# Differential attention on one core: one rope and one split per head, the lambda factor on ScalarE, and the head norms' reciprocal roots seeded by Ln and Exp

## Chip, cores and metric

The kernel runs on one core of one Trainium2 chip. The metric is the device time of one execution in microseconds, lower is better. The kernel before was run three times: median 1824.09 us, between 1821.87 and 1824.63 us.

## The reference

One step of a diffusion backbone of two layers, over 128 context tokens and 512 latent tokens (640 in all) of width 1024, with 256 cached context positions. Layer 0 runs gated linear attention (GLA, 4 heads) beside latent attention (MLA, 4 heads); layer 1 runs differential attention (8 heads, two maps of 64 dimensions each); each is followed by a gated MLP with a width-3 convolution. What the change touches is this:

```python
def rmsnorm(x, g):
    y = xf * lax.rsqrt(jnp.mean(xf * xf, axis=-1, keepdims=True) + EPS)
    return y * g
def diff_attend(q, k, v, lam, scale):       # blocks of 128 queries
    s = jnp.einsum('bqhnd,bkhnd->bnhqk', qb, k) * scale
    p = jax.nn.softmax(s, axis=-1)
    a = p[:, 0] - lam * p[:, 1]
    return jnp.einsum('bhqk,bkhv->bqhv', a, v)
def diff_output(o, w_out, d_gain, lam_init):
    o = rmsnorm(o, d_gain) * (1.0 - lam_init)   # per head
    return o.reshape(b, t, MIX_ODD) @ w_out
# latent queries and keys pass axial_rope; context ones and cached ones don't
# GLA's output is normed per head in the same way: rmsnorm(o, gla_gain) * silu(gate)
```

## The kernel before, in words

**Number format.** Every float32 operand is kept as a high and a low part; `split` (ACT cast at L172, DVE subtraction at L173) makes them out of an SBUF tile, `evict_split` (ACT L177, DVE L178) out of a PSUM tile, `W` out of a weight that a DMA brought (`wraw`: ACT cast `whi` at L163, subtraction `wlo` at L165, on POOL in the attention of layer 1, on DVE elsewhere). A product is three matmuls (`three`). Weights stay still and tokens stream through, so one projection of a tile of 128 output features (`proj_half`, L211) takes 24 matmuls for one half of the tokens (two halves, 320 each).

**Order of work.** The program is emitted stage by stage: adaLN, input projection, GLA with MLA's first units between, MLA, output projection, MLP, then layer 1: norm (`nm_t`, `B`), the differential attention, its output projection (begun within the last head), MLP. Inside a stage a scheduler sorts each engine's instructions again, from its own estimate of when each is ready, so an edit of a few instructions moves others. Each engine runs its queue in order.

**The head norms.** `rms_stats` (L264 on) has per-head sums of squares in PSUM (PE `rb`, L261) with 64 tokens on the partitions and 8 or 10 columns. DVE makes `rv` (mean plus epsilon, L266), takes an integer guess at the reciprocal root (L267, L268) and refines it in three Newton rounds of three instructions (L270 to L272): 12 DVE instructions, each on the one before. `rms_bc` then spreads the result: DVE `rdg` (L278), PE `rbc` (L282). It runs 12 times: five times on GLA's output (64x8; three within GLA, two at MLA's start) and for seven of the eight differential heads (64x10).

**Queries and keys of layer 1.** `unit_qk(kind, h, c)` (L1060) projects queries or keys of head `h` for the token half `c`: PE `qko` (L211), ACT copy into `fq` or `fk` (L1076), then `rope` of the latent columns (DVE shuffle L478, DVE product with the sine L479, POOL product with the cosine L480, DVE sum L481), then `split` into `qd` or `kd` (L172, L173). The first half holds 192 latent columns, the second 320. For keys, the cached 256 columns (`in_dkc`) have a split of their own.

**A head's jobs.** Five jobs of 128 queries (four latent ones against 768 keys, one context job against 128), for each: scores of both maps (PE `sc`, L826), the minimum per map (DVE `mn`, L851), the exponential with its row sums (ACT `p`, L852), and one job later the reciprocal of the sums (DVE L862), `diff_maps` (L1097 to L1099: DVE multiplies the second map's factor by lambda; ACT scales map 0; DVE adds map 1 times its factor), the transposes (PE `ptp`, L869), their eviction `pt` (L177, L178) and the product with the values (PE `pv`, L883). `diff_after` (L1107 on) takes the result and norms the finished head. Projections of the next head, `unit_qk` and values `vo` (L1046), are dealt out between the jobs as filling.

Of the kernel before, what the change touches and what calls it, by code (L numbers as in the profile page):

```python
# [12 lines left out]
I32 = mybir.dt.int32  # L13
ACTF = mybir.ActivationFunctionType
ALU = mybir.AluOpType
# [6 lines left out]
CTX = 128  # L22
LAT = 512
TOK = CTX + LAT
CUT = 320
PAST = 256
ALLK = TOK + PAST
# [29 lines left out]
def build(tc, a):  # L57
    nc = tc.nc
    V, S, G, PE = nc.vector, nc.scalar, nc.gpsimd, nc.tensor

    def pool(name, bufs=1, **kw):
        es = ExitStack()
        return es.enter_context(tc.tile_pool(name=name, bufs=bufs, reuse_waits="tile", **kw)), es
# [38 lines left out]
    for n, sh in SMALL:  # L102
        w = math.prod(sh)
        v = small[:, off:off + w]
        off += w
        if len(sh) == 2:
            v = v.rearrange("p (a b) -> p a b", b=sh[1])
        elif len(sh) == 3:
            v = v.rearrange("p (a b c) -> p a b c", b=sh[1], c=sh[2])
# [7 lines left out]
    lm, dgn, epst, lnh = scal[:, 0:4], scal[:, 4:5], scal[:, 5:6], scal[:, 6:7]  # L117
# [19 lines left out]
    class Weights:  # L137
# [23 lines left out]
        def split(self, raw, shape, eng=None):  # L161
            hi = self.tile("hi", shape, FP32R)
            S.copy(out=hi, in_=raw)  # L163
            lo = self.tile("lo", shape, FP32R)
            (eng or self.eng).tensor_tensor(out=lo, in0=raw, in1=hi.bitcast(FP32), op=ALU.subtract)  # L165
            return hi, lo
# [8 lines left out]
    def evict_split(dst, ps_ap, scale=None):  # L175
        if scale is None:
            S.copy(out=dst[0], in_=ps_ap)  # L177
            return V.tensor_tensor(out=dst[1], in0=ps_ap, in1=dst[0].bitcast(FP32), op=ALU.subtract)  # L178
        S.mul(out=dst[0], in_=ps_ap, mul=scale)
        return V.scalar_tensor_tensor(out=dst[1], in0=ps_ap, scalar=scale, in1=dst[0].bitcast(FP32),  # L180
                                      op0=ALU.mult, op1=ALU.subtract)

    def three(x, y):
        return ((x[0], y[0]), (x[0], y[1]), (x[1], y[0]))
# [30 lines left out]
    mark = {}  # L215
# [32 lines left out]
    def rms_stats(tp, bank, srcs, denom):  # L248
        sizes = [s[0].shape[-1] // 64 for s in srcs]
        nb = sum(sizes)  # L250
        sums = bank[0:64, 0:2 * nb].rearrange("p (c t) -> p c t", t=2)
        b0 = 0
        for parts, n in zip(srcs, sizes):
            acc = tp.tile([128, CUT], FP32, tag="racc", name="racc")[:, 0:64 * n]
            S.activation(out=acc, in_=parts[0], func=ACTF.Square)
            for s in parts[1:]:
                sq = tp.tile([128, CUT], FP32, tag="rsq", name="rsq", bufs=2)[:, 0:64 * n]
                S.activation(out=sq, in_=s, func=ACTF.Square)
                mark["acc"] = V.tensor_tensor(out=acc, in0=acc, in1=sq, op=ALU.add)
            for c in range(n):  # L260
                PE.matmul(out=sums[:, b0 + c], lhsT=acc[:, c * 64:(c + 1) * 64], rhs=negs[:, 0:2], start=True, stop=True)  # L261
            b0 += n
        y = tp.tile([64, 20], FP32, tag="ry", name="ry")[:, 0:nb]
        v = tp.tile([64, 20], FP32, tag="rv", name="rv")[:, 0:nb]  # L264
        t = tp.tile([64, 20], FP32, tag="rt", name="rt")[:, 0:nb]
        V.tensor_scalar(out=v, in0=sums[:, :, 0], scalar1=-1.0 / denom, scalar2=EPS, op0=ALU.mult, op1=ALU.add)  # L266
        V.tensor_scalar(out=t.bitcast(I32), in0=v.bitcast(I32), scalar1=1, scalar2=None, op0=ALU.logical_shift_right)  # L267
        V.tensor_scalar(out=y.bitcast(I32), in0=t.bitcast(I32), scalar1=-1, scalar2=0x5F3759DF, op0=ALU.mult, op1=ALU.add)  # L268
        for _ in range(3):
            V.tensor_tensor(out=t, in0=y, in1=y, op=ALU.mult)  # L270
            V.scalar_tensor_tensor(out=t, in0=t, scalar=-0.5, in1=v, op0=ALU.mult, op1=ALU.mult)
            V.scalar_tensor_tensor(out=y, in0=t, scalar=1.5, in1=y, op0=ALU.add, op1=ALU.mult)  # L272
        return y

    def rms_bc(tp, bank, y, bufs=1, after=None, tag="rdg"):
# [199 lines left out]
    def rope(tp, z, t0=0):  # L475
        n, t1 = z.shape[0], t0 + z.shape[-1]
        sh = tp.tile([n, LAT], FP32, tag="rsh", name="rsh")[:, t0:t1]
        V.stream_shuffle(sh, z, SHUF)  # L478
        V.tensor_tensor(out=sh, in0=sh, in1=ropeS[0:n, t0:t1], op=ALU.mult)  # L479
        G.tensor_tensor(out=z, in0=z, in1=ropeC[0:n, t0:t1], op=ALU.mult)  # L480
        V.tensor_tensor(out=z, in0=z, in1=sh, op=ALU.add)  # L481
# [48 lines left out]
    for j, (src, gain) in enumerate(((cqr, sm["qn"]), (ckr, sm["kvn"]))):  # L530
        for h, (c0, c1) in enumerate(CH):
            bc = rms(scp, ps("p1", "rb"), [src[:, i, c0:c1] for i in range(2)], 256)
            for i in range(2):
                last = V.scalar_tensor_tensor(out=src[:, i, c0:c1], in0=src[:, i, c0:c1], scalar=gain[:, i:i + 1], in1=bc,
                                              op0=ALU.mult, op1=ALU.mult)
# [164 lines left out]
    def stats(c):  # L700
        RY[c] = rms_stats(scp, ps("m", "rb"), [[z] for z in OO[c]], 128.0)
# [16 lines left out]
    for i in range(2):  # L718
        V.tensor_tensor_reduce(out=ljk, in0=lamp[:, 2 * i], in1=lamp[:, 2 * i + 1], op0=ALU.mult, op1=ALU.add,
                               scale=1.0, scalar=0.0, accum_out=lm[:, i:i + 1])  # L720
# [310 lines left out]
    un, ues = pool("un", side="left")  # L1031
    dqt, dkt, dvt, doh = {}, {}, {}, {}

    def diff_units(p):
        us = {}
        wv = []

        def unit_v(t):
            if t == 0:
                wv.extend(W(a["wvo"][p, i], [128, 4, 256]) for i in range(2))  # L1040
            vt = dvt[p, t] = [vp.tile([128, 256], FP32R, tag=f"vd{i}", name=f"vd{i}", bufs=9) for i in range(2)]
            o_ = ps("p1", "vo")[:, 0:256]
            for k in range(KT):
                lh = [z[:, k, t * 128:(t + 1) * 128] for z in B]
                for n, (l_, r_) in enumerate(three(lh, wv[k // 4])):
                    PE.matmul(out=o_, lhsT=l_, rhs=r_[:, k % 4], start=k == 0 and n == 0, stop=k == KT - 1 and n == 2)  # L1046
            evict_split(vt, o_)
            if t == 0:
                vf = un.tile([128, 256], FP32, tag="vf", name="vf")
                V.tensor_copy(out=vf, in_=o_)  # L1050
                nc.gpsimd.dma_start(out=a["o_dv"][:, p * 256:(p + 1) * 256], in_=vf)

        def unit_c():
            vc = un.tile([128, 2, 256], FP32, tag="vc", name="vc")
            nc.gpsimd.dma_start(out=vc, in_=a["dvc"][:, :, p * 256:(p + 1) * 256])
            for t in range(2):
                vt = dvt[p, 5 + t] = [vp.tile([128, 256], FP32R, tag=f"vd{i}", name=f"vd{i}", bufs=9) for i in range(2)]
                split(vc[:, t], vt[0], vt[1])

        hold = {}  # L1060

        def unit_qk(kind, h, c):
            isq = kind == "q"
            n = TOK if isq else ALLK
            if c == 0:
                w = W(a["wqo" if isq else "wko"][h], [128, KT, 128])
                f = kp.tile([128, ALLK], FP32, tag="qkf", name="f" + kind, bufs=2)
                t = [kp.tile([128, n], FP32R, tag=f"{kind}d{i}", name=f"{kind}d{i}", bufs=2) for i in range(2)]
                (dqt if isq else dkt)[h] = t
                hold[kind, h] = (w, f, t)  # L1070
                if not isq:
                    nc.gpsimd.dma_start(out=f[:, TOK:ALLK], in_=a["dkc"][:, h])
            w, f, t = hold[kind, h]
            c0, c1 = CH[c]
            o_ = proj_half(ps("p1", "qko"), w, B, KT, c)
            S.mul(out=f[:, c0:c1], in_=o_, mul=-DIFF_SCALE if isq else 1.0)  # L1076
            if c == 0 and not isq:
                nc.gpsimd.dma_start(out=a["o_dk"][:, h], in_=f[:, 0:CTX])
                split(f[:, TOK:ALLK], t[0][:, TOK:ALLK], t[1][:, TOK:ALLK])
            r0 = max(c0, CTX)  # L1080
            rope(un, f[:, r0:c1], r0 - CTX)
            split(f[:, c0:c1], t[0][:, c0:c1], t[1][:, c0:c1])

        for t in range(5):
            us[f"v{t}"] = lambda t=t: unit_v(t)
        us["c"] = unit_c
        for j in range(2):
            for kind in "qk":
                for c in range(2):
                    us[f"{kind}{j}{'ab'[c]}"] = lambda kind=kind, j=j, c=c: unit_qk(kind, 2 * p + j, c)  # L1090
        return us
# [2 lines left out]
        return [three([z[m * 64:m * 64 + 64] for z in dqt[h]], [z[m * 64:m * 64 + 64] for z in dkt[h]]) for m in range(2)]  # L1094

    def diff_maps(p, li, nk):
        V.tensor_scalar(out=li[:, 1:2], in0=li[:, 1:2], scalar1=lm[:, 2:3], scalar2=None, op0=ALU.mult)  # L1097
        S.mul(out=p[:, 0, 0:nk], in_=p[:, 0, 0:nk], mul=li[:, 0:1])
        V.scalar_tensor_tensor(out=p[:, 0, 0:nk], in0=p[:, 1, 0:nk], scalar=li[:, 1:2], in1=p[:, 0, 0:nk],  # L1099
                               op0=ALU.mult, op1=ALU.add)  # L1100
        return p[:, 0]
# [253 lines left out]
```

## Time and profile before

| | |
|---|---|
| median of 3 runs | 1824.09 us (1821.87 to 1824.63) |
| the profiled execution | 1819.55 us |
| its span in the profile | 1817.8 us |
| instructions | 29362 |
| mean granted TensorE clock | 0.98 |
| busy: PE, DVE, ACT, POOL | 1744.3, 1272.0, 758.9, 294.7 us |

The profile is of one execution, 4.5 us under the median; what lies outside its span is 1.75 us. PE is TensorE's matmuls, PEld its weight loads, DVE VectorE, ACT ScalarE, POOL GpSimd. Stages on the profile's clock: GLA some 175 to 275 us, MLA to 385, output projection and MLP to 900, layer 1's norm to 950, differential attention 950 to 1300, the rest to the end. The granted clock is a mean over a stretch, 1.00 being 2.4 GHz; TensorE runs at 2.4 or at 1.2 GHz.

### The profile page before, as it was taken

Reading aid. Unit: us, or ns where it says so; the run is one execution under the profiler, and the core shown is the slowest. Engines: PE = TensorE matmul, PEld = TensorE weight load, DVE = VectorE, ACT = ScalarE, POOL = GpSimd, SP = SyncE. Lnnn points to the kernel's source line nnn. Section 1 sums busy time; section 2 is a strip of 40 time slices with the busy share of each in tenths; the row PEclk is TensorE's granted clock in tenths of the full one; section 3 lists DMA queues with packets and bytes.
Section 4 is the critical chain, followed back from the end, with each engine's and each line's share of the span. In section 5 each row is a group of like instructions: output and inputs, shape, how many; then the busy total and the mean of one; then the engine's idle time right before and its main releaser. Section 6 shows DMA issues by size and latency. Waiting matters only on the chain. (4 is left out here: it accounts for less than half of the span.)

```text
span 1817.8 us, 29362 instructions
## 1 busy us (share of the span) xinstructions
PE 1744.3 (96%) x11716; PEld 1634.6 (90%) x11716; DVE 1272.0 (70%) x2438; ACT 758.9 (42%) x1344; POOL 294.7 (16%) x246
## 2 busy tenths in 40 slices
PE   7999989999999999999999999999999999999996
PEld 1898776889999999999988989897989999999996
DVE  5964877778699999946588787876475554545556
ACT  6444434544532232323356665665373232322232
POOL 3201021000310100100133232321031010101004
PEclk9999999999999999999999989998999999999998
DMA  9650001044256555412231021111122222222121
GB/s 372 198 166 9 28 3 72 4 175 139 93 174 189 171 176 184 156 59 88 65 123 61 31 58 42 63 49 70 59 70 81 82 70 79 73 73 79 59 82 58
DMA packets 57336, 176.58 MB, mean 97 GB/s; under 512 B 6064, under 2 KB 11568, under 8 KB 56816
## 3 DMA queue, kind: packets, MB, share of 16 engines
q1 hardware_dynamic: 53408, 160.59, 27.4%
q0 software_dynamic: 3792, 14.13, 2.2%
q8 instruction: 92, 1.51, 0.3%
q14 instruction: 44, 0.36, 0.1%
HBM read 166.59 MB, written 7.77 MB: 96 GB/s over the span
## 5 line engine op out<-in xcount | busy, mean ns | idle before, releaser
L202 PE MATMUL up<-B,whi 128*128 128x320 f32 x2560 | 479.6, 309 | 0.0
L163 ACT CAST whi<-wraw 128x1024 fp32r<-128x1024 f32 (+2 forms) x208 | 208.3, 1002 | 506.7 <-PE up L202 231.3
L202 PEld LDWEIGHTS up<-B,whi 128*128 128x128 f32 x2560 | 401.6, 188 | 0.0
L165 DVE TENSOR_TENSOR wlo<-wraw,whi 128x1024 fp32r<-128x1024 f32 (+2 forms) x175 | 204.2, 1167 | 226.3 <-ACT whi L163 226.0
L202 PE MATMUL up<-B,wlo 128*128 128x320 f32 x1280 | 291.8, 309 | 0.0
L202 PE MATMUL po<-A,whi 128*128 128x320 f32 x1312 | 246.3, 310 | 0.7 <-DVE u L967 0.5
L202 PEld LDWEIGHTS up<-B,wlo 128*128 128x128 f32 x1280 | 213.8, 188 | 0.0
L363 DVE CUSTOM_DVE_ANT_0 junk<-araw,cbc 128x1024 bf16<-128x1024 f32 x160 | 203.5, 1272 | 12.2 <-DMA araw<-in_wada0b 9.4
L202 PEld LDWEIGHTS po<-A,whi 128*128 128x128 f32 x1312 | 205.7, 188 | 1.5 <-issue 0.7
L173 POOL TENSOR_TENSOR A<-u,A 128x640 fp32r<-128x640 f32 x44 | 76.1, 1730 | 758.2 <-ACT A L172 733.2
L202 PE MATMUL po<-A,wlo 128*128 128x320 f32 x656 | 149.8, 310 | 0.5 <-DVE wlo L165 0.5
L211 PE MATMUL qko<-B,whi 128*128 128x320 f32 x512 | 121.6, 322 | 2.4 <-ACT B L172 1.5
L340 PE MATMUL pot<-A,whi 128*128 128x320 f32 x512 | 113.9, 312 | 0.0
L202 PEld LDWEIGHTS po<-A,wlo 128*128 128x128 f32 x656 | 109.5, 188 | 0.8 <-DVE wlo L165 0.8
L165 POOL TENSOR_TENSOR wlo<-wraw,whi 128x1024 fp32r<-128x1024 f32 x33 | 79.1, 2400 | 146.9 <-ACT whi L163 146.5
L965 DVE SCALAR_TENSOR_TENSOR u<-up,small,u 128x127 f32<-128x127 f32 (+1 forms) x176 | 95.5, 543 | 10.4 <-ACT u L963 9.5
L967 DVE SCALAR_TENSOR_TENSOR u<-up,small,u 128x127 f32<-128x127 f32 (+1 forms) x176 | 96.3, 548 | 4.5
L852 ACT ACTIVATE p<-sc,mn 128x768 f32<-128x768 f32 (+1 forms) x100 | 79.2, 797 | 39.8 <-DVE mn L851 39.3
L211 PEld LDWEIGHTS qko<-B,whi 128*128 128x128 f32 x512 | 89.0, 196 | 5.2 <-ACT B L172 1.8
L851 DVE TENSOR_REDUCE mn<-sc 128x1 f32<-128x768 f32 (+1 forms) x100 | 79.3, 816 | 16.1 <-PE sc L826 15.3
L340 PEld LDWEIGHTS pot<-A,whi 128*128 128x128 f32 x512 | 85.7, 188 | 1.1 <-issue 0.4
L202 PE MATMUL pe<-B,whi 128*128 128x320 f32 x416 | 81.2, 317 | 4.3 <-DVE nm_t L306 3.6
(294 smaller groups left out, 3056.0 us busy)
## 6 DMA issues: line engine op xcount, KB each, us to landing
wraw<-in_wup SPq DMA_DIRECT2D x88, 512.0 KB, 3.6
araw<-in_wada SPq DMA_DIRECT2D x48, 512.0 KB, 3.4
wraw<-in_wdn SPq DMA_DIRECT2D x40, 512.0 KB, 3.6
araw<-in_wada0b SPq DMA_DIRECT2D x32, 512.0 KB, 4.3
wraw<-in_wie SPq DMA_DIRECT2D x13, 512.0 KB, 4.4
aw<-in_wada0a SPq DMA_DIRECT2D x8, 512.0 KB, 8.8
wraw<-in_wada0a SPq DMA_DIRECT2D x8, 512.0 KB, 8.0
wraw<-in_woe SPq DMA_DIRECT2D x8, 512.0 KB, 4.3
```

The lines of the kernel that those rows point to most:

```text
L163: S.copy(out=hi, in_=raw)
L165: (eng or self.eng).tensor_tensor(out=lo, in0=raw, in1=hi.bitcast(FP32), op=ALU.subtract)
L173: return (lo_eng or V).tensor_tensor(out=lo, in0=src, in1=hi.bitcast(FP32), op=ALU.subtract)
L202: PE.matmul(out=o, lhsT=w[wi][:, k], rhs=hl[ri][:, k, c0:c1], start=k == 0 and n == 0, stop=k == nk - 1 and n == 2)
L211: PE.matmul(out=o, lhsT=w[wi][:, k], rhs=hl[ri][:, k, c0:c1], start=k == 0 and n == 0, stop=k == nk - 1 and n == 2)
L340: PE.matmul(out=o, lhsT=ws[j + m][wi][:, k], rhs=hl[ri][:, k, c0:c1], start=k == 0 and n == 0, stop=k == nk - 1 and n == 2)
L363: V.tensor_tensor_reduce(out=junk, in0=raw, in1=self.cbc[:, j], op0=ALU.mult, op1=ALU.add, scale=1.0, scalar=0.0, accum_out=mods[l][:, t0 ...
L851: V.tensor_reduce(out=mn[:, m:m + 1], in_=ss[m][:, 0:nk], op=ALU.min, axis=AX.X)
L852: self.exp = S.activation(out=p[:, m, 0:nk], in_=ss[m][:, 0:nk], func=ACTF.Exp, scale=-1.0, bias=mn[:, m:m + 1], accum_out=li[:, m:m + 1])
L965: V.scalar_tensor_tensor(out=u[:, s0 + 1:s1], in0=r[:, s0:s1 - 1], scalar=cw[:, 0:1], in1=u[:, s0 + 1:s1], op0=ALU.mult, op1=ALU.add)
L967: last = V.scalar_tensor_tensor(out=u[:, s0:s1 - 1], in0=r[:, s0 + 1:s1], scalar=cw[:, 2:3], in1=u[:, s0:s1 - 1], op0=ALU.mult, op1=ALU.add)
```

## The change

Three edits. In `rms_stats` the two integer instructions and two of the three Newton rounds go; ACT computes the start as Ln and then Exp with a scale of -0.5, and one round stays. In `unit_qk` the rope and the split are issued once per head and kind, when both halves are there: the rope over 512 columns, the split over 640 for queries and over 896 for keys (the cached columns with them). In `diff_maps` the lambda factor is an ACT instruction instead of a DVE one.

```diff
@@ rms_stats
-        V.tensor_scalar(out=t.bitcast(I32), in0=v.bitcast(I32), scalar1=1, scalar2=None, op0=ALU.logical_shift_right)
-        V.tensor_scalar(out=y.bitcast(I32), in0=t.bitcast(I32), scalar1=-1, scalar2=0x5F3759DF, op0=ALU.mult, op1=ALU.add)
-        for _ in range(3):
-            V.tensor_tensor(out=t, in0=y, in1=y, op=ALU.mult)
-            V.scalar_tensor_tensor(out=t, in0=t, scalar=-0.5, in1=v, op0=ALU.mult, op1=ALU.mult)
-            V.scalar_tensor_tensor(out=y, in0=t, scalar=1.5, in1=y, op0=ALU.add, op1=ALU.mult)
+        with tc.issue_after(mark["tab"].ins):
+            S.activation(out=t, in_=v, func=ACTF.Ln)
+            S.activation(out=y, in_=t, func=ACTF.Exp, scale=-0.5)
+        V.tensor_tensor(out=t, in0=y, in1=y, op=ALU.mult)
+        V.scalar_tensor_tensor(out=t, in0=t, scalar=-0.5, in1=v, op0=ALU.mult, op1=ALU.mult)
+        V.scalar_tensor_tensor(out=y, in0=t, scalar=1.5, in1=y, op0=ALU.add, op1=ALU.mult)
@@ unit_qk
             if c == 0 and not isq:
                 nc.gpsimd.dma_start(out=a["o_dk"][:, h], in_=f[:, 0:CTX])
-                split(f[:, TOK:ALLK], t[0][:, TOK:ALLK], t[1][:, TOK:ALLK])
-            r0 = max(c0, CTX)
-            rope(un, f[:, r0:c1], r0 - CTX)
-            split(f[:, c0:c1], t[0][:, c0:c1], t[1][:, c0:c1])
+            if c == 1:
+                rope(un, f[:, CTX:TOK])
+                split(f[:, 0:n], t[0], t[1])
@@ diff_maps
-        V.tensor_scalar(out=li[:, 1:2], in0=li[:, 1:2], scalar1=lm[:, 2:3], scalar2=None, op0=ALU.mult)
+        S.mul(out=li[:, 1:2], in_=li[:, 1:2], mul=lm[:, 2:3])
```

`mark["tab"]` orders Ln and Exp behind the load of the activation table that both are in; the number of table loads is the same in both kernels. The changed file is one line shorter, so lines from L1083 on are one less there: the lambda factor is L1096, ACT's scaling of map 0 L1097, DVE's sum L1098. PE has the same matmuls in another order. Three places of its queue show it.

PE at MLA's start, where the last GLA chunk's norm is spread (`rbc`) among MLA's projections (`uq`, `uv`) and products with values (`pv`). Before:

```order
L883 MATMUL pv<-pt_2780,B_65 128x256
L883 MATMUL pv<-pt_2781,B_65 128x256
L883 MATMUL pv<-pt_2780,B_65 128x256 x2
L883 MATMUL pv<-pt_2781,B_65 128x256
L883 MATMUL pv<-pt_2780,B_65 128x256
L282 MATMUL rbc<-rdg,negs 128x256 x2
L795 MATMUL uv<-wv_2674,B_66 128x256
```

In the change:

```order
L282 MATMUL rbc<-rdg,negs 128x256
L211 MATMUL uq<-cqn_1570,whi 128x320
L211 MATMUL uq<-cqn_1571,whi 128x320
L211 MATMUL uq<-cqn_1570,wlo 128x320
...
L883 MATMUL pv<-pt_2751,B_65 128x256
L883 MATMUL pv<-pt_2750,B_65 128x256
L282 MATMUL rbc<-rdg,negs 128x256
L795 MATMUL uv<-wv_2644,B_66 128x256
```

The two `rbc` stood next to each other behind `pv`; now six `uq` and nine `pv` stand between them.

PE at the entry of the differential attention, where the first head's scores (`sc`; `kd` and `qd` with the two numbers are the high and low parts of its keys and queries) stand among the projections `qko` of the second head's keys. Before:

```order
L211 MATMUL qko<-B_65,wlo 128x320
L826 MATMUL sc<-kd_9143,qd_9233 128x512 x2
L211 MATMUL qko<-B_65,wlo 128x320
L826 MATMUL sc<-kd_9144,qd_9233 128x512 x2
L826 MATMUL sc<-kd_9143,qd_9234 128x512 x2
L826 MATMUL sc<-kd_9143,qd_9233 128x256 x2
L826 MATMUL sc<-kd_9144,qd_9233 128x256 x2
L826 MATMUL sc<-kd_9143,qd_9234 128x256 x2
L211 MATMUL qko<-B_65,whi 128x320
L211 MATMUL qko<-B_66,whi 128x320
```

In the change:

```order
L211 MATMUL qko<-B_65,whi 128x320
L211 MATMUL qko<-B_66,whi 128x320
L211 MATMUL qko<-B_65,wlo 128x320
L826 MATMUL sc<-kd_9113,qd_9194 128x512 x2
L826 MATMUL sc<-kd_9114,qd_9194 128x512 x2
L826 MATMUL sc<-kd_9113,qd_9195 128x512 x2
L826 MATMUL sc<-kd_9113,qd_9194 128x256 x2
L826 MATMUL sc<-kd_9114,qd_9194 128x256 x2
L826 MATMUL sc<-kd_9113,qd_9195 128x256 x2
L826 MATMUL sc<-kd_9113,qd_9194 128x512
L826 MATMUL sc<-kd_9114,qd_9194 128x512
```

Before, 22 of the 46 `qko` stood behind the first job's first scores, 21 of them between the first job and the second. Now all 46 stand ahead of the first score, and 30 `sc` (the first job's 12, the second's 12, half of the third's) follow one another.

PE at the end of a head (here the second; the fourth and sixth have the same), behind the context job's scores and the norm's `rbc`. Before:

```order
L282 MATMUL rbc<-rdg,negs 128x320 x2
L826 MATMUL sc<-kd_10378,qd_10600 128x512
L826 MATMUL sc<-kd_10379,qd_10600 128x512
L826 MATMUL sc<-kd_10378,qd_10601 128x512
L826 MATMUL sc<-kd_10378,qd_10600 128x256
L826 MATMUL sc<-kd_10379,qd_10600 128x256
L826 MATMUL sc<-kd_10378,qd_10601 128x256
L869 MATMUL ptp<-small,p 128x128 x3
```

In the change:

```order
L282 MATMUL rbc<-rdg,negs 128x320 x2
L869 MATMUL ptp<-small,p 128x128 x6
L883 MATMUL pv<-pt_10650,vd_10127 128x256
L211 MATMUL qko<-B_65,whi 128x320
L211 MATMUL qko<-B_66,whi 128x320
```

Where 12 `sc` of the next head's first job stood, there are now the transposes, a `pv` and 22 `qko`; the scores follow behind them.

## Rows read from the trace of the kernel before

**Rows 1.** The page: busy time by engine, and the chain that ended last by engine.
```profile
PE 1744.3 (96%) x11716; PEld 1634.6 (90%) x11716; DVE 1272.0 (70%) x2438; ACT 758.9 (42%) x1344; POOL 294.7 (16%) x246
PE 40%; DVE 4%; ACT 3%; issue 1%; DVEq 0%; ACTq 0%
```

**Rows 2.** Windows by stage. Columns: window, its length, busy time (instructions) of PE, PEld, DVE, ACT and POOL, granted clock, DMA share, GB/s.
```profile
175.00:275.00 100.00, 90.73 (x746) 72.74 (x745) 79.74 (x208) 41.83 (x99) 15.89 (x18) 1.00 0.06 19
900.00:950.00 50.00, 46.47 (x307) 44.14 (x306) 42.91 (x93) 29.73 (x67) 14.20 (x18) 0.97 0.30 105
950.00:975.00 25.00, 23.18 (x146) 21.20 (x145) 21.10 (x39) 15.90 (x31) 9.73 (x9) 0.86 0.16 52
975.00:1235.00 260.00, 252.90 (x1870) 231.88 (x1868) 205.77 (x475) 157.79 (x350) 78.39 (x64) 0.97 0.16 50
1235.00:1300.00 65.00, 59.17 (x355) 52.77 (x354) 35.36 (x79) 29.16 (x63) 5.27 (x9) 0.87 0.19 65
```

**Rows 3.** Short windows, same columns: one of GLA, and five of the differential attention (its entry, and places at the end of heads).
```profile
200.00:225.00 25.00, 22.86 (x189) 18.56 (x187) 22.53 (x59) 12.54 (x29) 0.00 (x0) 1.00 0.00 1
960.00:972.00 12.00, 10.18 (x58) 9.29 (x57) 10.30 (x19) 9.94 (x19) 4.18 (x3) 0.72 0.13 44
1052.00:1060.00 8.00, 6.00 (x48) 5.29 (x48) 7.07 (x12) 3.56 (x9) 4.25 (x4) 0.88 0.51 163
1064.00:1076.00 12.00, 11.48 (x55) 9.41 (x54) 9.50 (x22) 7.16 (x18) 3.52 (x2) 0.72 0.16 45
1138.00:1148.00 10.00, 7.99 (x60) 7.36 (x57) 9.31 (x22) 5.18 (x12) 3.69 (x4) 0.83 0.33 107
1220.00:1228.00 8.00, 7.08 (x54) 6.38 (x55) 6.95 (x19) 4.65 (x12) 2.96 (x2) 0.84 0.33 104
```

**Rows 4.** Timeline of DVE in GLA, a norm's Newton instructions among GLA's own. Columns here and in the other timelines: start in us, duration in us, engine, line, operation; in brackets the idle time before it and what ended it.
```profile
224.48 0.15 DVE L270 TENSOR_TENSOR rt<-ry 64x8 f32<-64x8 f32 x1
224.56 0.72 DVE L667 COPY_PREDICATED sT<-lmask,gp 128x512 f32<-128x512 uint32 x1
225.55 0.16 DVE L270 TENSOR_TENSOR rt<-ry 64x8 f32<-64x8 f32 x1
225.74 0.16 DVE L271 SCALAR_TENSOR_TENSOR rt<-rt,rv 64x8 f32<-64x8 f32 x1
```

**Rows 5.** Timelines of DVE and of PE at MLA's start, the last GLA chunk's norm.
```profile
296.75 0.16 DVE L266 TENSOR_SCALAR rv<-rb 64x8 f32<-64x8 f32 x1 [0.31 <-PE rb L261]
299.90 0.42 DVE L278 TENSOR_TENSOR rdg<-nid,ry 64x256 f32<-64x256 f32 x1
300.38 0.70 PE L282 MATMUL rbc<-rdg,negs 64*128 64x256 f32 x2 [0.73 <-DVE rdg L278]
301.97 0.69 PE L282 MATMUL rbc<-rdg,negs 64*128 64x256 f32 x2 [0.90 <-DVE rdg L278]
```

**Rows 6.** Timeline of the entry of the differential attention, the first two jobs of the first head and the wait ahead of the third.
```profile
954.38 0.50 PE L826 MATMUL sc<-kd,qd 64*128 64x512 f32 x2
956.91 1.81 DVE L851 TENSOR_REDUCE mn<-sc 128x1 f32<-128x768 f32 x2
957.89 0.90 ACT L852 ACTIVATE p<-sc,mn 128x768 f32<-128x768 f32 x1 [2.05 <-DVE mn L851]
959.43 1.90 PE L826 MATMUL sc<-kd,qd 64*128 64x512 f32 x12
963.15 3.31 PE L826 MATMUL sc<-kd,qd 64*128 64x512 f32 x12 [1.82 <-ACT p L852]
```

**Rows 7.** First PE's waits from 900 to 1310 us (line, what it waited for: us in total, times, longest), then rows of the timeline at ends of heads.
```profile
PE pv L883 <- DVE pt L178: 6.7, 5, 2.0
PE sc L826 <- ACT p L852: 4.3, 6, 1.8
985.77 1.30 PE L826 MATMUL sc<-kd,qd 64*128 64x512 f32 x6 [0.86 <-ACT p L852]
1053.02 3.48 DVE L1099 SCALAR_TENSOR_TENSOR p<-p,li 128x768 f32<-128x768 f32 x1 [0.93 <-ACT p L1098]
1053.32 2.36 POOL L165 TENSOR_TENSOR wlo<-wraw,whi 128x1024 fp32r<-128x1024 f32 x1
1067.41 1.51 PE L826 MATMUL sc<-kd,qd 64*128 64x512 f32 x6 [0.52 <-ACT p L852]
1152.85 1.31 PE L826 MATMUL sc<-kd,qd 64*128 64x512 f32 x6 [0.52 <-ACT p L852]
```

**Rows 8.** Groups of instructions by form from 944 to 1290 us. Columns: line, engine, operation, names, shapes, count; busy us, mean ns; idle us before them and what ended it.
```profile
L1097 DVE TENSOR_SCALAR li<-li,scal 128x1 f32<-128x1 f32 x40 | 8.4, 211 | 0.8
L1099 DVE SCALAR_TENSOR_TENSOR p<-p,li 128x768 f32<-128x768 f32 x32 | 42.4, 1326 | 14.3 <-ACT p L1098 14.1
L479 DVE TENSOR_TENSOR rsh<-rsh,ropeS 128x320 f32<-128x320 f32 x16 | 17.6, 1097 | 0.1
```

**Rows 9.** One line's instructions over the whole span, those whose size the change uses or comes near to. Columns: line, engine, operation, count; duration in ns (lowest, median, highest); first and last start in us; shapes.
```profile
L478 DVE STREAM_SHUFFLE rsh<-qrf x2: 724/734/743, 273.9 to 318.3; 128x512 f32<-128x512 f32 x2
L480 POOL TENSOR_TENSOR qrf<-qrf,ropeC x2: 1284/1289/1294, 274.7 to 319.1; 128x512 f32<-128x512 f32 x2
L173 DVE TENSOR_TENSOR krs<-kr,krs x1: 1093/1093/1093, 118.1 to 118.1; 128x896 fp32r<-128x896 f32 x1
L172 ACT CAST csr<-csil x1: 206/206/206, 6.7 to 6.7; 128x16 fp32r<-128x16 f32 x1
```

## The prediction, made before the changed kernel was run

> **What bounds the kernel now.** I read the page first: PE is busy 96% of the span, and the chain that ended last lies on PE far more than on any other engine [rows 1]. So an instruction taken from DVE or ACT is worth nothing by itself; it is worth what PE stands still for it. Next the windows by stage, for where PE does stand still [rows 2]. In GLA it is busy 90.7 us of 100, and DVE there 22.5 of 25 us in a typical stretch [rows 3]: DVE sets the pace. In the differential attention PE has 252.9 of 260 us, DVE 205.8: PE sets the pace, and DVE only at places. PE loses there in two ways: 7 us idle, and the granted clock, 0.97 of full speed on average and 0.86 and 0.87 at entry and end. A stretch's clock loss I take as (1 - granted clock) x length: at the lower of its two levels, 1.2 GHz, the engine needs twice as long. Last the waits of PE and the timelines at those places [rows 5 to 7], to see whose work ends them.
>
> **The change, part by part.** The sum is made against the profiled execution, 1819.55 us, and carried over to the median, 1824.09; the two are 4.5 us apart, so the difference counts, not the profile's own time.
>
> *Newton rounds in GLA.* Three norms lose 8 of 12 DVE instructions each. One standing alone behind another starts 0.19 us after it; one slipped behind a long instruction of another chain adds 0.08 (it starts at 224.48 and the next at 224.56) [rows 4]. With half of each kind that is 8 x 0.13 = 1.05 us, three times 3.1. DVE is the engine that sets the pace, so I count all of it: -3.1. The bounds are 0 (the chunk's chain runs over ACT's exponentials anyway) and 3 x 8 x 0.19 = -4.6. Ln and Exp stand on ACT behind exponentials that are due earlier and ahead of casts; ACT is busy 41.8 of 100 us [rows 2] and covers them; without that cover, two at the 0.206 us of a small cast [rows 9] would cost 0.4 a norm.
>
> *MLA's start.* The norm of the last chunk is a bare chain here: from `rv` at 296.75 to `rdg` at 299.90 it is 3.15 us, and PE waits 0.73 and 0.90 for the two `rdg` [rows 5]. Without 8 links of 0.19 and with two of 0.2 the chain is 1.1 us shorter or more, and the new order puts six `uq` and nine `pv` between the two spreads. Both waits go: -1.6. The bounds are 0, if something else is late at the same places, and -2.7, if the 1.1 us come on top. Layer 1's norm is not touched; its stage has 3.5 us of PE idle [rows 2], and its order shifts a little: 0, plus or minus 1.
>
> *Entry of the differential attention.* Now the first score starts at 954.38, the 21 projections behind the first job cover its minima and exponentials, the second job starts at 959.43 without a wait, and only the third waits, 1.82 us [rows 6]. In the new order all 46 projections come first and nothing stands between the jobs. The 22 that move forward take as long in front as behind, and cover the whole rope and the longer splits, so the first score starts near 957.5 and nothing is lost yet. Then the scores of a map need their PSUM tile back, which the job before frees by minimum and exponential. Ahead of the second job PE waits for a shuffle of the next head's rope (0.73) [rows 9], two minima (1.81 together) and an exponential (0.90) [rows 6], 3.5 in all, less 1.1 that lie beside the scores' own second half: 2.4. Ahead of the third, DVE also has the rest of that rope and the 896-column split of the keys (1.09), the sine product held up by POOL's cosine product of 1.29 [rows 9] as it is now with 320 columns, which take 1.10 [rows 8]: 3.2. A last wait makes 0.3. Together 5.9 instead of 1.8: **+4.1**. The bounds: 0, if the scheduler's order is right and the engines are ready; and three waits of the full 2.7 (two minima and one exponential) and the 0.73, 8.8 less 1.8: +7.0. Behind today's wait the clock falls: 0.72 over 12 us, 3.4 us lost [rows 3]. Two longer waits may bring it down twice; I take half of a second such loss, **+1.7**, between 0 and +3.4.
>
> *Ends of heads.* PE waits 0.86, 0.52 and 0.52 for the context job's exponential, as the next scores need its PSUM tile [rows 7]. In the new order transposes, a `pv` and projections stand there at the last two and something like it at the first: the waits are filled, -1.9. After the second of them the clock is at 0.72 for 12 us [rows 3]; if the wait is what lets it fall, that comes back too, **-3.4**; the bounds are 0 and -3.4. The other waits, 6.7 us for the eviction of the transposes [rows 7], I leave. The DVE sum at L1099 takes 3.48 us in front of that eviction instead of 1.33 on average [rows 7, 8], because POOL's `wlo` of 2.36 runs at the same time, and the change moves neither. The longer key split and the lambda instruction now stand in front, +0.2 each at three places: +0.6.
>
> *Lambda and the rest.* DVE loses 40 lambda instructions, 8.4 us [rows 8], seven norms' 8 links, and some work of the two-part ropes. All of that lies under PE's 252.9 of 260 us [rows 2] and I cost it at nothing. If PE's cover breaks at some job, the freed DVE time is a gain, not a loss; ACT's side is a rival below. The last head, where the clock is 0.87 [rows 2], has a new order too: 0, plus or minus 2.
>
> The sum: -3.1 - 1.6 + 4.1 + 1.7 - 1.9 - 3.4 + 0.6 = **-3.6 us**, 1820.5 as a median.
>
> **The lambda factor and a rule.** For a small ACT instruction this case has 0.206 us [rows 9], for the DVE one 0.211 [rows 8]: by the rows the move is even, and what counts is which queue it stands in. The Trainium skill, page "ScalarE: Activation LUTs", section "Rules for kernel authors", says of products: "Use VectorE, not ScalarE". The same page, section "What ACT_TABLE_LOAD costs", gives an ACTIVATE 186 ns and 93 ns more for each per-partition operand: an estimate of 0.28 us here, 40 x 0.28 = 11 us instead of the 8.2 of the last rival if all lay on the path. By that rule the edit should be undone; no row of this kernel shows the form itself.
>
> **Rivals.**
>
> *Larger gain.* The waits for the eviction go as well, since DVE has fewer instructions in its queue at the ends of heads, and with them the clock losses there: 8 x 0.12 + 10 x 0.17 + 8 x 0.16 = 4.0 us [rows 3]. Then -3.6 - 0.6 - 6.7 - 4.0 = -14.9: 1809.2. For it: DVE is busy 7.07 of 8 us and 9.31 of 10 there. Against: what delays the eviction is the one slow sum beside POOL, which stays.
>
> *It does nothing that counts.* The scheduler places the work so that what DVE gives back in GLA is waited for at ACT's exponentials, while entry and ends cancel as forecast: -3.6 + 3.1 = -0.5, 1823.6. For it: PE is at 96%, and each gain hangs on a place of 0.5 to 1 us.
>
> *Slower at the entry.* The one mechanism is the chain of three jobs of scores without filling. If every job waits the full chain, +7.0, and each wait is followed by a stretch at the lower clock, +3.4, and no gain comes at the ends (+0.6): -4.7 + 7.0 + 3.4 + 0.6 = +6.3, 1830.4. It decides once the waits at the entry pass about 6 us in all. For it: the order has nothing between the scores, and the clock now falls behind one wait of 1.8 us. Against: it is one place in the program, and later heads keep their filling.
>
> *Slower by ACT's queue.* The lambda factor stands between the second exponential and the scaling of map 0, for which the DVE sum already waits 14.1 us [rows 8]. If each of 40 goes straight into PE's time at 0.206 us, that is +8.2 on the forecast: +4.6, 1828.7. Against: PE has other work at most of these places.
>
> **How the numbers follow.** Forecast 0.50, larger gain 0.13, nothing 0.15, slower at the entry 0.17, slower by ACT 0.05. The forecast's own range is 1815 to 1825: the clock's 3.4 at the ends and the entry's 4.1 can each fail to come. The whole range, 1810 to 1831, takes in all but the far half of the larger gain and the upper half of the slower entry. A measurement of this kernel can tell about 0.2%, 3.6 us, from no change. The forecast lies on that edge: of its 0.50 I put 0.28 on faster and 0.22 on same; the larger gain adds 0.13 to faster; the third case gives 0.11 to same and 0.02 to each side; the slow ones 0.21 to slower and 0.01 to same. Faster 0.43, same 0.34, slower 0.23.
>
> **What would show it.** In the changed kernel's profile: GLA's stage about 3 us shorter with DVE still near 90%; no wait of `rbc` for `rdg` at MLA's start; the first score some 3 us later on the stage's own clock and two waits of `sc` for `p` between 2 and 3.5 us behind it; no such wait behind the context jobs of heads two and four; waits of `pv` for `pt` still near 2 us. The prediction is wrong in its mechanism if GLA keeps its length, if the entry has no wait longer than today's, or if the change of time lies in the stages in front of or behind 175 to 1300 us.

## The result: slower where the forecast had faster

The changed kernel takes 1831.90 us (median of 6 runs, 1829.26 to 1837.21); the kernel before, run again beside it, 1821.83 us (6 runs). The ratio is 1.0061, 95% interval 1.0041 to 1.0081: some 11 us slower where 3.6 us faster was forecast, and 0.9 us above the range. Its profiled execution took 1830.81 us, span 1829.0 us, mean granted clock 0.979 against 0.980.

The windows by stage of the changed kernel, with the columns of [rows 2]:

```profile
175.00:275.00 100.00, 93.28 (x755) 74.75 (x754) 75.92 (x183) 43.38 (x108) 14.97 (x19) 1.00 0.07 20
950.00:975.00 25.00, 20.56 (x106) 17.77 (x105) 17.07 (x24) 16.37 (x31) 7.82 (x6) 0.73 0.12 33
975.00:1235.00 260.00, 249.76 (x1828) 227.70 (x1826) 178.05 (x309) 159.29 (x363) 73.29 (x49) 0.97 0.16 50
1235.00:1300.00 65.00, 58.26 (x326) 50.20 (x325) 34.77 (x68) 31.82 (x77) 7.89 (x10) 0.83 0.14 49
```

DVE gave back 28 us in the long window, and PE did not get any: it is busy less, not more. In GLA it is busy 2.5 us more in the same 100 us, which is part of the gain ahead of layer 1.

Windows with fixed ends mix the stages once a kernel runs ahead or behind, so the stages are better measured from the first and the last instruction of a line. For the changed kernel (line, operation, count; ns lowest/median/highest; first and last start; shapes):

```profile
L826 PE MATMUL sc<-kd,qd x432: 269/383/792, 951.6 to 1271.3; 64*128 64x256 f32 x65, 64*128 64x512 f32 x63, 64*128 64x128 f32 x16
L950 PE MATMUL po<-A,whi x96: 303/309/555, 1245.7 to 1303.9; 128*128 128x320 f32 x96
L202 PE MATMUL up<-B,whi x2560: 309/309/309, 473.9 to 1783.7; 128*128 128x320 f32 x197
```

The same rows of before begin or end at 954.4, 1292.5 and 478.8 to 1772.5 us. GLA's first matmul starts at 183.6 us instead of 182.4. So from there to the first MLP matmul the change gains 6.1 us; from the first differential score to the last output projection it loses 14.2 (338.1 to 352.3), and 3.2 more, as the 22 projections moved ahead of that first score are no longer in it; the rest is even.

Within the differential stage I split the time in three, the same way for each trace: PE's waits (the brackets of its timeline), the clock's loss ((1 - granted clock) x length, in windows of 4 us), and what is left.

| profile | stage | waits | clock | left |
|---|---|---|---|---|
| before | 338.1 | 14.2 | 20.4 | 303.5 |
| the change | 352.3 | 21.2 | 25.6 | 305.5 (+3.2) |

So of 17.4 us there, 7.0 are waits, 5.2 clock, and 5.2 neither. The waits of PE from 900 to 1310 us, which answer to the first two of [rows 7]:

```profile
PE sc L826 <- ACT p L852: 5.8, 4, 2.6
PE ptp L869 <- DVE pt L178: 3.8, 8, 0.6
PE pv L883 <- ACT pt L177: 3.2, 4, 1.0
PE qko L211 <- DVE doh L1124: 2.1, 2, 1.2
PE po L950 <- ACT A L172: 2.0, 1, 2.0
PE pv L883 <- DVE pt L178: 1.7, 3, 0.6
```

The 6.7 us behind the slow DVE sum fell to 1.7, and new lines stand there: transposes wait for evictions, projections for the norm (`doh`), products with the values for ACT.

One name has to be set right before these places are read. What the section on the change calls the end of the second head (and of the fourth and sixth) is where the third, fifth and seventh head run their last jobs; the norm that PE spreads there (`rbc`) is that of the second, fourth and sixth head. Below, the place goes by the head whose jobs end there.

### The profile page after: what moved, and what is told of

It reads as the page before. It is cut to its first block, busy times and chain, and to the rows that moved or that the text cites. A ratio compares the mean times of both kernels' runs of the same rounds, so it can differ in the third digit from the quotient of the medians.

```text
span 1829.0 us, 29148 instructions
## 1 busy us (share of the span) xinstructions
PE 1752.2 (96%) x11716; PEld 1638.8 (90%) x11716; DVE 1241.8 (68%) x2214; ACT 768.7 (42%) x1384; POOL 288.1 (16%) x230
```

## Experiments

Each was timed in five rounds beside the kernel before; the difference is that of the medians. The change itself, counted the same way, stands at +10.1.

| run | edit against before | ratio (95%) | us |
|---|---|---|---|
| e1_ln | Ln and Exp only | 0.9949 (0.9931 to 0.9967) | -9.4 |
| e2_rope | merged rope and split only | 1.0122 (1.0100 to 1.0144) | +22.7 |
| e3_lam | lambda on ACT only | 1.0042 (1.0026 to 1.0059) | +8.2 |
| e4_lnlam | both ACT edits | 0.9963 (0.9946 to 0.9980) | -6.8 |
| e5_head0 | the change, first head in halves | 1.0070 (1.0046 to 1.0095) | +14.0 |
| e6_lnrope | the change, lambda on DVE | 1.0098 (1.0075 to 1.0121) | +19.3 |
| e7_pair_after | the change, scores in turns | 1.0100 (1.0076 to 1.0124) | +18.5 |
| e8_ln_pair | e1, scores in turns | 0.9976 (0.9962 to 0.9990) | -5.0 |
| e9_qonly | the change, only queries merged | 1.0094 (1.0077 to 1.0111) | +18.1 |
| e10_konly | the change, only keys merged | 0.9983 (0.9970 to 0.9997) | -3.1 |
| e11_ropelam | merged, and lambda on ACT | 1.0116 (1.0098 to 1.0133) | +22.4 |
| e12_ln_gla | Ln and Exp for GLA's norms only | 0.9961 (0.9947 to 0.9975) | -5.4 |
| e13_ln_fill | e1 with matmuls in three waits | 0.9914 (0.9897 to 0.9932) | -16.7 |
| e14_ln_nolam | e1 without lambda | 0.9945 (0.9925 to 0.9965) | -11.3 |
| e15_qfirst | the change, queries dealt out first | 1.0158 (1.0134 to 1.0182) | +28.2 |

### Which edit: e1 to e4

The edits are those of the diff, one or two at a time.

> The Ln and Exp seed alone, rope, split and lambda as before. Theory 1 (the merged rope and split make the loss, through a new order of PE's queue in the differential attention): only the gain in GLA and at MLA's start is left, about 6 us in the two traces, the differential stage keeps its 338 us from the first score to the last output projection; about 6 us faster than before. Theory 2 (ACT is late: the added ACT instructions delay the exponentials and the evictions at the ends of heads): the same 6 us gained, 4 or more of them lost at the ends of heads; within 2 us of before.

> One rope and one split per head alone, norms and lambda as before. Theory 1: the whole loss of the differential stage without the gain ahead of it, entry +6, ends of heads +5, scores of the two maps run apart +4: some 14 to 17 us slower than before, first wait of scores behind the first job near 2.6 us. Theory 2: the entry's 6 only, since ACT has no new instruction here: about 6 us slower, and no wait of products with the values for an ACT eviction.

> The lambda factor on ACT alone. Theory 1: no more than 2 us either way, the order of PE's scores hardly differs from before (14 jobs of 768 keys paired, as before). Theory 2: 40 instructions of some 0.2 us in ACT's queue, 4 to 8 us slower, waits of products with the values for ACT's eviction at the ends of heads.

> Both ACT edits, the rope and split in halves as before. Theory 1: about 6 us faster than before, as with Ln and Exp alone. Theory 2: the gain of 6 eaten by ACT's delays, within 3 us of before or slower.

The merge is the loss, +22.7 us, more than theory 1 had. Ln and Exp gain 9.4, more than the 6 ahead of the differential stage: that stage is 5.2 us shorter too (332.9 us). Of these 22.7 us, 19.0 lie in the differential stage (357.1 us): 5.6 more of waits and 13.7 more of clock loss. Theory 2 had the size of lambda, which costs 8.2 us by itself; the 2.6 beside Ln and Exp lie within the two intervals. In e3_lam, lambda's line on ACT (columns as above):

```profile
L1097 ACT ACTIVATE li<-li,scal x40: 282/296/321, 962.3 to 1270.2; 128x1 f32<-128x1 f32 x40
```

and who waited there for the scaling of map 0 behind it (us, times):

```profile
  DVE p L1099: 21.6, 26
```

One takes 0.296 us where I put the 0.206 of a small cast, and the sum waits 21.6 us instead of 14.1 [rows 8]. PE's waits in the stage hardly rise (14.2 to 14.7 us), and the waits for ACT's eviction that theory 2 expected are not among them; the clock loss rises (20.4 to 25.6).

### Where: e5 to e8

```diff
 e5: unit_qk of the change
+            if h == 0:          # cached split, rope and split by halves, as before
...
+            elif c == 1:
                 rope(un, f[:, CTX:TOK])
                 split(f[:, 0:n], t[0], t[1])
 e6: diff_maps of the change
-        S.mul(out=li[:, 1:2], in_=li[:, 1:2], mul=lm[:, 2:3])
+        V.tensor_scalar(out=li[:, 1:2], in0=li[:, 1:2], scalar1=lm[:, 2:3], scalar2=None, op0=ALU.mult)
 e7, e8: s_stage of the change and of e1
+            prev = None
             for grp in zip(*ops):
                 for f in grp:
-                    mark["att"] = f()
+                    with tc.issue_after(prev.ins) if prev and nm == 2 else ExitStack():
+                        prev = mark["att"] = f()
```

> The change, but the first head's queries and keys keep rope and split in halves, so that PE's queue at the entry is the one of before (22 of 46 projections behind the first job's first scores); the ends of heads stay as in the change. Theory 1 (the entry costs its waits, 2.6 us more, and a longer stretch at the low clock, 3.4 us more): about 6 us faster than the change, near 1826 us, no wait of scores longer than 2 us at the entry. Rival (the loss is at the ends of heads alone, and the clock falls there instead when it does not at the entry): within 2 us of the change.

> The change with the lambda factor on DVE as before. Alone the lambda edit cost some 8 us in time; theory 1: its 40 instructions of 0.29 us lie in front of the scaling of map 0 in every job here too, 6 us or more faster than the change, near 1826. Rival: at the ends of heads PE waits for ACT's eviction and the merged splits anyway, lambda is covered by these, within 2 us of the change.

> The change, with each differential job's scores held in the order map 0, map 1, map 0, ... by ordering edges alone, so that no other work stands between the maps and neighbours come from different maps. Theory 1 (a job whose maps run apart takes PE 2.5 us, a job in turns 1.3): score matmuls some 10 us less PE time, 4 to 10 us faster than the change. Rival: map 0's scores now wait until both PSUM tiles of the job before are free, 0.9 us a job behind the second exponential, which eats the gain: no faster, and waits of scores for the exponential in most of the 32 jobs.

> Ln and Exp alone, with the same ordering edges on the scores. Theory 1: the same gain on the faster kernel, 4 to 10 us below Ln and Exp alone, near 1803. Rival: waits for the exponential eat it, 1810 or more.

All four missed theory 1, and e6 missed its rival too. In e5 the entry was mended: its window, and the one wait of PE's timeline that is left there:

```profile
950.00:975.00 25.00, 23.51 (x134) 20.69 (x133) 16.52 (x26) 16.25 (x32) 10.06 (x7) 0.80 0.19 59
```

```profile
958.09 2.28 PE L826 MATMUL sc<-kd,qd 64*128 64x512 f32 x6 [1.49 <-ACT p L852]
```

PE waits 1.49 us in all instead of 4.4, and the stage's waits fall from 21.2 to 17.1 us. Yet the time is that of the change: the stage's clock loss is 32.4 us in this profile, 25.6 in the change's. The entry was the largest price in my sum, and undoing it bought nothing that shows (the two intervals leave room for some 4 us, not for the 6 of theory 1). In e6 lambda back on DVE is some 7 to 9 us slower than the change, by intervals that just touch, and not faster; e11 beside e2 shows no difference between the two. So what lambda costs depends on the rest. In e7 and e8 the scores in turns are slower by 0.4% and 0.3% than without: now PE waits 2.63 and then 2.65 us at the entry and 1.87 us at three spreads of the norm in e7. The waits of scores in most of the 32 jobs, which the rival had, are not there (4 in e7, 6 in e8). All of PE's waits in the stage grow instead, from 21.2 us in the change to 30.8 in e7 and from 13.1 in e1 to 21.1 in e8, most of them at other instructions than scores; that the second map's late tile holds these back is not shown.

### Which half of the merge: e9, e10, e15

```diff
 e9: unit_qk of the change
+            if not isq:         # keys by halves, as before; queries merged
 e10:
+            if isq:             # queries by halves, as before; keys merged
 e15: the filling's order, both merged
-    even_plan = ["k1a", "v3 k1b", "v4 c q1a", "q1b", ""]
-    odd_plan = ["k0a", "k0b", "q0a v0", "q0b v1", "v2"]
+    even_plan = ["q1a", "v3 q1b", "v4 c k1a", "k1b", ""]
+    odd_plan = ["q0a", "q0b", "k0a v0", "k0b v1", "v2"]
```

> The change with only the queries' rope and split merged; keys keep their halves and the cached split of their own. Theory 1 (a merged query rope makes the next head's first job wait for the second half of its queries, so that its scores move behind the transposes and projections at the ends of heads): PE's queue at the ends is that of the change, and so is the time, 8 to 12 us slower than before. Rival (the 896-column key split is the late one): as fast as without any merging, about 7 us faster than before.

> The change with only the keys' rope and split merged. Theory 1: PE's queue at the ends of heads is that of before, waits there as with both ACT edits alone; some 4 us for the entry, whose keys come later, so 2 to 5 us faster than before. Rival (the key split): as slow as the change, 10 us slower than before.

> The merged rope and split with the lambda factor on ACT, norms as before. Rope alone gave +22 us, lambda alone +8. If the two add, +30 us; if lambda on ACT helps where rope and split are merged, as the change beside the change without lambda seems to say (6 us), +16; no difference would be +22.

> Ln and Exp for the five GLA norms alone, the seven head norms of the differential attention with three Newton rounds as before. If the 9 us of Ln and Exp come from GLA and MLA's start, as the stages' lengths say for 6 of them, 6 us or more are kept; the rest belongs to the seven head norms, where 8 fewer links on DVE move the norm's spread and what waits for it.

> The change with the filling's order turned: queries' halves of the next head first, keys' halves last, both still merged. Theory 1 (what hurts is that the operand dealt out last becomes whole only with its second half): the keys take the queries' place, the ends of heads wait as in the change, 8 us or more slower than before. Rival (the queries as such): the keys are no harm, as with only the keys merged, 2 to 5 us faster than before at the ends, the entry aside.

With only the keys merged the kernel is 3.1 us faster than before, 3.7 behind the two ACT edits alone. With only the queries merged it is as slow as the change, or slower: +18.1 us, where 8 to 12 were expected. PE's timeline at the end of the third head, e9 first, then e10:

```profile
1068.53 0.52 PE L869 MATMUL ptp<-small,p 128*128 128x128 f32 x3 [0.64 <-DVE pt L178]
1069.45 0.52 PE L869 MATMUL ptp<-small,p 128*128 128x128 f32 x3 [0.40 <-DVE pt L178]
1071.66 0.56 PE L211 MATMUL qko<-B,whi 128*128 128x320 f32 x2 [1.58 <-DVE doh L1130]
```

```profile
1066.21 1.32 PE L826 MATMUL sc<-kd,qd 64*128 64x512 f32 x6 [0.22 <-ACT p L852]
```

Three waits, 2.6 us in all, where e10 has one of 0.22, at the place where [rows 7] has 0.52. The next head's first job takes queries 128 to 255 only, which lie in the first half. Merged, it needs the second half's projection, rope and split, and the queries are dealt out last; the keys, a job or two earlier, have time. In e15 the keys come last, and the same place of it reads:

```profile
1082.97 0.52 PE L869 MATMUL ptp<-small,p 128*128 128x128 f32 x3 [0.63 <-DVE pt L178]
1083.89 0.87 PE L869 MATMUL ptp<-small,p 128*128 128x128 f32 x3 [0.40 <-DVE pt L178]
1085.78 0.90 PE L211 MATMUL qko<-B,whi 128*128 128x320 f32 x2 [0.81 <-DVE doh L1124]
```

The same waits with keys in the queries' place: the harm is that of the operand dealt out last. (The 28 us of e15 are not all of this: its first head has waits of 2.1 to 3.8 us of its own, and the stage's clock loss is 44.0 us where the change has 25.6.) e12 says that 5.4 of the 9.4 us of Ln and Exp come from GLA and MLA's start, a little less than the 6 expected; e11, as slow as e2, says that beside the merge alone lambda on ACT neither adds nor helps.

### What a wait costs, and lambda left out: e13, e14

```diff
 e13: rms_stats of e1, four more matmuls behind the second part's sums
+            for _ in range(more if b0 else 0):      # more = 4 for heads 1, 3, 5, else 0
+                PE.matmul(out=bank[:, 128:128 + 64 * n], lhsT=negs, rhs=acc, start=True, stop=True)
 e14: diff_maps of e1
-        V.tensor_scalar(out=li[:, 1:2], in0=li[:, 1:2], scalar1=lm[:, 2:3], scalar2=None, op0=ALU.mult)
```

> Ln and Exp alone, with four matmuls of 320 columns, whose result nobody reads, put behind the norm's sums of the second, fourth and sixth head, where PE stands 2.0, 2.0 and 0.9 us for the eviction behind the slow DVE sum. Theory 1 (a wait costs twice: its idle time and then a stretch at the low clock, here 1.7 to 3.4 us at each of the three places): the waits are filled, the clock stays at 1.00 behind them, 3 to 7 us faster than Ln and Exp alone, near 1805. Rival (the low clock comes anyway, with these waits or elsewhere): the matmuls only add to PE's queue, same as Ln and Exp alone or up to 5 us slower.

> Ln and Exp alone, with the lambda factor left out (map 1 is subtracted with its own factor, so the output is not the reference's). Theory (DVE's 40 lambda instructions of 0.21 us lie under PE): within 2 us of Ln and Exp alone, so that what lambda costs on ACT, 2.6 us beside Ln and Exp and 8 alone, is ACT's queue. Rival: DVE's lambda is on the path in front of its sum, 4 us or more faster.

e13 is the fastest kernel of all, 1803.83 us, 6.5 under e1, by doing more. PE's timeline in e1 at the three places, then windows of 10 us at all three, columns as in [rows 3]:

```profile
1047.87 0.74 PE L261 MATMUL rb<-negs,racc 128*64 128x2 f32 x10
1050.62 1.76 PE L883 MATMUL pv<-pt,vd 128*128 128x256 f32 x8 [2.01 <-DVE pt L178]
1131.92 1.46 PE L883 MATMUL pv<-pt,vd 128*128 128x256 f32 x9 [2.01 <-DVE pt L178]
1212.12 2.29 PE L883 MATMUL pv<-pt,vd 128*128 128x256 f32 x9 [0.93 <-DVE pt L178]
```

```profile
1048.00:1058.00 10.00, 7.99 (x53) 7.89 (x53) 8.43 (x19) 3.75 (x10) 1.59 (x2) 0.83 0.17 57
1129.00:1139.00 10.00, 7.99 (x52) 7.77 (x53) 8.72 (x19) 3.68 (x10) 1.88 (x2) 0.83 0.22 68
1209.00:1219.00 10.00, 9.07 (x57) 8.70 (x58) 8.93 (x19) 4.97 (x13) 2.11 (x2) 0.66 0.17 55
```

The same in e13, the timeline at the first place only:

```profile
1048.25 0.74 PE L261 MATMUL rb<-negs,racc 128*64 128x2 f32 x10
1048.93 2.42 PE L263 MATMUL rb<-racc,negs 128*128 128x320 f32 x8
1051.01 2.22 PE L885 MATMUL pv<-pt,vd 128*128 128x256 f32 x16
```

```profile
1047.00:1057.00 10.00, 10.00 (x76) 9.05 (x76) 8.76 (x16) 4.84 (x14) 2.96 (x3) 1.00 0.30 92
1127.00:1137.00 10.00, 10.00 (x75) 9.05 (x75) 8.72 (x17) 4.84 (x13) 2.87 (x2) 1.00 0.25 92
1206.00:1216.00 10.00, 10.00 (x77) 8.78 (x76) 8.16 (x17) 5.45 (x14) 2.70 (x2) 1.00 0.21 68
```

The added matmuls take 2.08 us until the next starts, the wait 2.01: nothing is gained there, and 1.1 us are lost at the third place, where the wait was 0.93. What is gained is the clock: 1.00 instead of 0.83, 0.83 and 0.66, which is 1.7 + 1.7 + 3.4 = 6.8 us, and the run gains 6.5. All six executions of e13 have a mean granted clock of 0.984 or more, none of e1's six more than 0.982. So at these three places a wait of PE of 1 to 2 us cost itself and nearly as much again, at the third place more than three times as much, in matmuls at the lower of the two levels behind it. e14 leaves lambda out and stays at e1's time: on DVE those 40 instructions were free, as forecast.

## Why the prediction was wrong

*GLA and MLA's start: right in sum.* -4.7 forecast, -6.1 in the profile; the division was not. GLA, for which -3.1 was forecast, is 0.8 us shorter by its `ep` matmuls and 1.8 by its last `op`; the rest comes in MLA and its projection. The two waits of `rbc` for `rdg` fell from 1.6 to 0.2 us, as forecast.

*Entry: right in sum, and undoing it bought nothing.* +4.1 of waits and +1.7 of clock were forecast. PE's timeline at the entry of the changed kernel:

```profile
955.64 3.14 PE L826 MATMUL sc<-kd,qd 64*128 64x512 f32 x12 [2.63 <-ACT p L852]
960.60 2.29 PE L826 MATMUL sc<-kd,qd 64*128 64x512 f32 x6 [1.81 <-ACT p L852]
```

That is 4.4 instead of 1.82, +2.6, and the window's clock loss is 25 x 0.27 = 6.8 instead of 3.5, +3.3; together +5.9 for the 5.8 forecast, by luck, since the waits came out 1.5 us under and the clock 1.6 over. The slower rival had this place for its mechanism and came out near the measured time (1830.4), by luck too: in e5, with 1.5 us of these waits left, the kernel is as slow.

*Ends of heads: the step that failed.* The prediction read in the order that transposes, `pv` and projections "stand there", and concluded "the waits are filled", -1.9, and that the clock "comes back too", -3.4. Before, PE's waits at the end of the third head were the 0.52 of [rows 7] and, 10 us ahead of it:

```profile
1057.30 1.62 PE L883 MATMUL pv<-pt,vd 128*128 128x256 f32 x9 [2.00 <-DVE pt L178]
```

There the changed kernel's PE did this:

```profile
1055.33 0.39 PE L883 MATMUL pv<-pt,vd 128*128 128x256 f32 x1 [0.75 <-ACT pt L177]
1056.08 0.74 PE L261 MATMUL rb<-negs,racc 128*64 128x2 f32 x10 [0.36 <-ACT racc L255]
1057.41 1.33 PE L883 MATMUL pv<-pt,vd 128*128 128x256 f32 x9 [0.59 <-DVE pt L178]
1066.09 0.52 PE L869 MATMUL ptp<-small,p 128*128 128x128 f32 x3 [0.63 <-DVE pt L178]
1067.01 0.52 PE L869 MATMUL ptp<-small,p 128*128 128x128 f32 x3 [0.40 <-DVE pt L178]
1068.90 0.65 PE L211 MATMUL qko<-B,whi 128*128 128x320 f32 x2 [1.25 <-DVE doh L1124]
```

Each of the fillers waits for something itself: the transposes for the eviction that frees their tile, the projections for the norm that frees theirs. That makes 3.98 us at this head for 2.52 before, and over all ends 12.6 for 7.8: +4.8 where -1.3 was forecast (with the +0.6). The clock there came out even (8.5 us lost before, 8.6 in the change, from 1050 to 1250 us), not -3.4. I had asked what stands in the wait's place and not whether it is ready. And I had costed the merge by its instructions, at nothing, and not by what it makes late; e9 and e10 show that this is the whole of the loss and more: merging the queries costs it, merging the keys at most some 4 us.

*The waits for the eviction: left as they were, and they fell.* The prediction left the 6.7 us, since the change would not move the slow DVE sum beside POOL's `wlo`. It did move it. In the change, at the same place:

```profile
1054.62 2.27 DVE L1098 SCALAR_TENSOR_TENSOR p<-p,li 128x768 f32<-128x768 f32 x1 [0.88 <-ACT p L1097]
1053.68 2.38 POOL L165 TENSOR_TENSOR wlo<-wraw,whi 128x1024 fp32r<-128x1024 f32 x1
```

The sum now starts 0.9 us behind `wlo` and shares 1.4 us with it; in [rows 7] it started ahead and shared all 2.4. It takes 2.27 us instead of 3.48, and PE's wait of 2.00 became one of 0.59. So the waits that the larger-gain rival had go did mostly go, 6.7 to 1.7 us in the stage, though not for its reason; the new waits at the ends, the 0.75 and 0.36 us above among them, took more than that gave.

*Lambda: right on DVE, mis-sized on ACT.* 0.296 us, not 0.206, and 8.2 us by itself, where 0.05 of the chance stood. The Trainium skill, page "ScalarE: Activation LUTs", section "Rules for kernel authors", would have kept the product on VectorE; e3 and e14 agree with it, e4 leans the same way within the noise, and e6 and e11 do not show it where rope and split are merged. The prediction's estimate of 0.28 us, from the same page of the Trainium skill, section "What ACT_TABLE_LOAD costs", is close to the 0.296 measured.

*Neither waits nor clock, 5.2 us: not foreseen.* The scores of a job's two maps overlap on PE when they are neighbours. Two jobs of before, in turns and one map behind the other, then one of the change with projections between the maps:

```profile
975.60 1.33 PE L826 MATMUL sc<-kd,qd 64*128 64x512 f32 x12
1085.94 1.90 PE L826 MATMUL sc<-kd,qd 64*128 64x512 f32 x12
```

```profile
1088.60 1.31 PE L826 MATMUL sc<-kd,qd 64*128 64x512 f32 x6
1091.07 1.31 PE L826 MATMUL sc<-kd,qd 64*128 64x512 f32 x6
```

Split, the next instruction starts 1.24 us behind each, 2.48 a job, for 1.83 unsplit. PE's order has 11 such jobs in the change and 4 before: 7 x 0.65 = 4.6 us, an estimate that fits the 5.2 left over. It holds as far as the jobs that run in turns or back to back make up for each other between the two orders. No run shows it as a cause: e7 and e8 removed all splitting and paid more in waits.

**What stays open.** The edits do not add: -9.4, +22.7 and +8.2 make +21.5, the change has about +11. Between profiles with no more waits the stage's clock loss differs by some 7 us (the change 25.6, e5 32.4, e6 32.5). A good part of that may be chance: the granted clock differs between executions of one kernel. The change's six run from 1829.26 us at a mean of 0.979 to 1837.21 at 0.971, e5's seven from 1827.12 at 0.981 to 1838.60 at 0.974, and the change was profiled at 0.979, e5 at 0.974. At 0.974 both take about 1835 us or more, at 0.979 to 0.980 both about 1830. e6's five lie between 0.971 and 0.974, and why it is lower I cannot say from the traces. So the 5.2 us of clock in the split of the change's loss are those of one execution. e13 shows that waits bring the low clock, not which wait does in which kernel.

## What to carry to other kernels

Before merging two instructions into one, look who needs the first half alone, and how long before the second is there: an operand that is dealt out last becomes whole last, and what begins on its first part then begins late. Work that a new order puts into a wait fills it only if it is ready itself, tiles included. On a kernel that PE bounds, price a wait of PE of a microsecond or two at twice its length or more (here the differential stage's clock loss was 1.0 to 1.9 times its waits, over the profiles of all 17 kernels); where it can't be taken away, a few matmuls of no use in it may pay.

## What the runs showed that I had not expected

- Twelve matmuls of 320 columns (24 records in the trace) whose result is not used made the kernel 6.5 us faster (e13 against e1), all of it from the granted clock: the differential stage's clock loss fell from 17.1 to 8.5 us.
- A [128 x 1] product with a per-partition factor takes 0.296 us on ACT and 0.211 on DVE.
- Twelve score matmuls of 64 rows take 1.3, 1.9 or 2 x 1.3 us on PE, by whether the two maps are in turns, back to back or parted.
